# Pooling units side by side, and other places for the gate units' loads, one S4 product and the pooling weights

## The chip, the core and the metric

The kernel runs on one NeuronCore of one Trainium2 chip. The metric is the device time of one execution in microseconds; lower is better. TensorE (PE) multiplies matrices into PSUM, VectorE (DVE) and ScalarE (ACT) do the elementwise work, GpSimd (POOL) and SyncE (SP) mostly issue transfers (DMAs). Each engine has a queue of its own and works it off in the order in which it was written when the program was built; engines wait for each other, and for transfers, on semaphores.

## The reference

One layer of a sequence model: 512 positions, 1024 channels, float32.

```python
h = rms_norm(x, norm_mix)
u_pool, u_lru, q, k, v, g_logits = split(h @ w_in)        # 1024 columns each, g_logits 3 x 1024
gates  = sigmoid(g_logits + b_gate)                       # three branches
y_pool = per group g (windows 2, 4, 8, 16):  (mean over window - u) @ w_pool[g], times pool_scale
y_lru  = width-4 conv, two block-diagonal gates, a scan over positions
y_sb   = stick-breaking attention, 8 heads of 128, strictly causal
merged = gates0 * (y_pool @ w_branch0) + gates1 * (y_lru @ w_branch1) + gates2 * (y_sb @ w_branch2)
x = x + merged @ w_out
x = x + (silu(h2 @ w_ffn_gate) * (h2 @ w_ffn_up)) @ w_ffn_down
```

## The kernel before, in words

**Precision.** Every float32 factor is split into a high part (ACT copies it to `float32r`) and a low part (DVE subtracts), and a product is three matmuls: high with high, high with low, low with high (`mm3`, `product`). The weight halves `whi`, `wlo` have three buffers each, filled by `split_w` (lines 142 and 143).

**Seven products for eight.** The columns of `w_in` for v, k, q, for the pooling input and for the third branch's gates are multiplied by a seven-product scheme (Strassen's, in Winograd's form). A *unit* is one such 2 x 2 block problem; its seven products are called 11, 12, 21/22 sums S1 to S4, and 22. The sums of activations (T1 to T4) are made once. The sums of weights are made partly by GpSimd transfers that add in flight (`accum_op=ALU.add`, lines 197, 212, 242, 249) and partly by DVE (lines 206 and 211). For a pooling unit (`add_pool7`) the buffer "21" first receives block 21 plus block 22 (S1); when S1 has been split, block 11 is added to it (S2); when S2 has been split, block 12 is added (S4). Buffer "11" receives block 21 after product 11 has been split, which gives S3. So S1, S2 and S4 of one unit are a chain: split, added transfer, split, added transfer, split.

**The stages, in time.** After the first gates and the LRU projections come v, k and q (three units of large products, line 858), then the two pooling units (`cc` 0 and 1, products `ps_uy`, `ps_ux`), then the two units of the third branch's gates (units 3 and 4, products `ps_gy`, `ps_gx`; all of these at line 342). In the stage before, unit 0 of the pooling runs all its seven products, then unit 1. Each pooling unit has two PSUM pairs, Y and X, of four pairs in all. A running mean of each pooling half (`pool_mean`, DVE, lines 933 to 941) is queued in a background list `bg`, of which `tick` issues a piece after each product.

Then follow the branches: `branch(1, c)` (LRU output `yHH`, `yHL`, loaded by GpSimd at line 1250 into the buffers that held the activations) and `branch(0, c)` (pooling output), four chunks `c` each, two weight halves per chunk. The pooling's own small products (`pool_back`, `pps`) stand ahead of them in the program. Attention's 52 steps (`abg`, from `queue_attention`: per head a load, transposes, scores, weights' transposes, output) are spread between: each `tick` issues the next step. In the kernel before, `pool_back` ticks eight times, a chunk half of either branch ticks 1 + 2 times (`TICKS`), and `branch(0, c)` once more ahead of each chunk. After the branches comes the third branch's seven-product part (`b7`), the output projection and the FFN.

**What sets the order.** The text of the program gives each instruction a priority; `tc.high_priority(n)` moves a piece ahead by n instructions. When the program is built, a planner with its own cost estimates writes each engine's queue from these priorities, and it also chooses which freed buffer a new tile takes. `weights(key)` makes the splits of up to two products beyond the one in use. A transfer whose buffer is not yet free, or whose source is not yet written, holds up everything behind it in the queue of the engine that issues it.

**Buffers.** The pooling and gate blocks lie in eight buffers of tag "w" (`NAW`); unit 1's gate temporaries `gx1`, `gy1` take two of the same. Branch weights come in through three buffers of tag "raw" in the pool `wp`, and in the kernel before the pooling group weights `rawp` (line 1045) go through the same three, two groups at a time. The later stages have twelve load slots (`slot_ld`, tag "l") on the memory that the "w" buffers held before.

## Time and profile before

| | us |
|---|---|
| median of the runs | 901.07 (900.61 to 902.67, 3 runs) |
| profiled execution | 898.37 |
| its span, first to last instruction | 896.6 |
| PE busy | 867.5 (97%) |
| DVE busy | 745.3 (83%) |
| ACT busy | 528.5 (59%) |
| POOL busy | 96.6 (11%) |

The span is what the trace covers; the execution's own time is 1.8 us longer. Busy time of PE is counted over pipelined matmuls, so 97% doesn't mean that the array worked at its full rate: the granted clock (PEclk) has to be read beside it. The profile names instructions by their line and by out<-in of tile names without numbers, so `pw<-in_w_pool_dram` is a load or an added transfer of pooling blocks, and `qw<-in_w_gate_dram` one of a gate unit. `DVE pw` at lines 933 to 941 is a running mean, which happens to have the same name.

### The profile page before, as it was taken

What the parts mean: (1) busy time and instruction counts of PE and PEld (TensorE: products, weight loads), DVE (VectorE), ACT (ScalarE), POOL (GpSimd) and SP (SyncE); (2) the same over time, 40 slices, a digit from 0 to 9 for tenths busy, and PEclk for the clock granted to TensorE, in tenths of its full rate; (3) what the DMA queues carried; (4) which work ended last, traced back from release to release, by engine and by line L of the source; (5) the groups of instructions that cost most, each with busy time, mean ns of one, the idle gap of its engine ahead of it and who ended that gap; (6) DMA issues with size and microseconds to landing.
All of it is one profiled execution on the core that took longest, in us unless ns stands there. A gap on an engine that the chain in (4) does not pass through costs nothing.

```text
span 896.6 us, 14576 instructions
## 1 busy us (share of the span) xinstructions
PE 867.5 (97%) x5707; PEld 796.3 (89%) x5707; DVE 745.3 (83%) x947; ACT 528.5 (59%) x733; POOL 96.6 (11%) x139
## 2 busy tenths in 40 slices
PE   9999999999968988999999999999999999999998
PEld 6888878888858987879888998889999999999998
DVE  6799898989746874897998597689988889899974
ACT  6554998667834464776765454446555555755642
POOL 1110002232351012000000110000000000021300
PEclk9999999999979999999999999999999999999999
DMA  9586255998787638844564685427444333698923
GB/s 339 144 293 189 95 187 165 280 264 231 237 239 186 161 104 283 258 138 145 161 180 144 130 197 189 130 82 212 119 108 139 108 94 119 184 255 205 198 54 118
DMA packets 114725, 158.31 MB, mean 177 GB/s; under 512 B 8288, under 2 KB 86112, under 8 KB 114656
## 3 DMA queue, kind: packets, MB, share of 16 engines
q1 hardware_dynamic: 100832, 107.30, 37.4%
q0 software_dynamic: 13680, 49.81, 24.4%
q8 instruction: 45, 0.74, 0.3%
q10 hardware_dynamic: 144, 0.26, 0.1%
q14 instruction: 24, 0.20, 0.1%
HBM read 136.90 MB, written 18.87 MB: 174 GB/s over the span
## 4 chain that ended last, share of the span: by engine, by line
PE 79%; DVE 8%; ACT 5%; DMA 5%; issue 2%; POOL 0%; SPq 0%; DVEq 0%; ACTq 0%; POOLq 0%
PE ps_y L342 11%; PE ps_x L342 8%; PE ps_q L858 7%; PE ps_dy L1710 6%; PE ps_dx L1710 5%; DMA pw<-in_w_pool_dram 3%; PE ps_gate L761 3%; PE ps_bY L1334 2%; DVE wlo L143 2%; PE ps_br L334 2%; PE ps_br L335 2%; PE ps_br L333 2%; PE ps_gy L342 2%; PE ps_bX L1334 2%; PE ps_uy L342 2%
## 5 line engine op out<-in xcount | busy, mean ns | idle before, releaser
L142 ACT ACTIVATE whi<-raw 128x1024 fp32r<-128x1024 f32 x61 | 64.4, 1056 | 73.4 <-PE ps_out L334 15.5
L143 DVE TENSOR_TENSOR wlo<-raw,whi 128x1024 fp32r<-128x1024 f32 x61 | 74.3, 1219 | 25.7 <-ACT whi L142 25.4
L143 DVE TENSOR_TENSOR wlo<-qw,whi 128x1024 fp32r<-128x1024 f32 x48 | 58.2, 1217 | 17.5 <-ACT whi L142 17.5
L142 ACT ACTIVATE whi<-qw 128x1024 fp32r<-128x1024 f32 x48 | 50.4, 1053 | 32.9 <-PE ps_q L858 11.8
L1495 ACT ACTIVATE wh_S<-w_S 128x1024 fp32r<-128x1024 f32 x36 | 38.2, 1062 | 29.0 <-PE ps_y L342 20.4
L1616 POOL DMA_DIRECT2D dw<-in_w_down_dram x20 | 17.3, 883 | 304.4 <-DMA dw<-in_w_down_dram 253.3
L1496 DVE TENSOR_TENSOR wl_S<-w_S,wh_S 128x1024 fp32r<-128x1024 f32 x36 | 43.8, 1219 | 3.3 <-ACT wh_S L1495 3.3
L1495 ACT ACTIVATE wh<-w 128x1024 fp32r<-128x1024 f32 x27 | 28.7, 1062 | 27.7 <-PE ps_x L342 9.4
L1496 DVE TENSOR_TENSOR wl<-w,wh 128x1024 fp32r<-128x1024 f32 x27 | 32.9, 1220 | 7.9 <-ACT wh L1495 7.9
L1495 ACT ACTIVATE whdS<-dw 128x1024 fp32r<-128x1024 f32 x20 | 21.2, 1058 | 20.4 <-PE ps_dy L1710 10.6
L143 DVE TENSOR_TENSOR wlo<-pw,whi 128x1024 fp32r<-128x1024 f32 x14 | 16.6, 1221 | 18.5 <-ACT whi L142 18.5
L1496 DVE TENSOR_TENSOR wldS<-dw,whdS 128x1024 fp32r<-128x1024 f32 x20 | 24.1, 1219 | 4.9 <-ACT whdS L1495 4.9
L333 PE MATMUL ps_br<-yHH,whi 128*128 128x512 f32 x64 | 24.4, 384 | 2.6 <-DVE gy L921 1.3
L1141 DVE TENSOR_TENSOR_SCAN E<-K,ahead 128x512 f32<-128x512 f32 (+3 forms) x32 | 25.3, 812 | 1.4 <-ACT K L1137 1.4
L334 PE MATMUL ps_br<-yHL,whi 128*128 128x512 f32 x64 | 24.7, 386 | 1.8 <-DMA yHL<-ydl 1.8
L333 PE MATMUL ps_lru<-HH,whi 128*128 128x512 f32 x64 | 24.6, 384 | 0.0
L333 PE MATMUL ps_br<-yph,whi 128*128 128x512 f32 x64 | 24.5, 383 | 0.0
L335 PE MATMUL ps_br<-yHH,wlo 128*128 128x512 f32 x64 | 24.5, 383 | 0.0
L333 PE MATMUL ps_gate<-HH,whi 128*128 128x512 f32 x64 | 24.4, 381 | 0.0
L334 PE MATMUL ps_lru<-HL,whi 128*128 128x512 f32 x64 | 24.3, 379 | 0.0
L335 PE MATMUL ps_lru<-HH,wlo 128*128 128x512 f32 x64 | 24.3, 379 | 0.0
L334 PE MATMUL ps_gate<-HL,whi 128*128 128x512 f32 x64 | 24.3, 379 | 0.0
(778 smaller groups left out, 3551.6 us busy)
## 6 DMA issues: line engine op xcount, KB each, us to landing
qw<-in_w_qkv_dram SPq DMA_DIRECT2D x24, 512.0 KB, 7.5
raw<-in_w_in_dram SPq DMA_DIRECT2D x23, 512.0 KB, 5.2
dw<-in_w_down_dram POOLq DMA_DIRECT2D x20, 512.0 KB, 8.1
w<-in_w_ffn_gate_dram SPq DMA_DIRECT2D x36, 256.0 KB, 4.2
w<-in_w_ffn_up_dram SPq DMA_DIRECT2D x36, 256.0 KB, 4.7
raw<-in_w_branch_dram SPq DMA_DIRECT2D x16, 512.0 KB, 4.1
qw<-in_w_qkv_dram POOLq DMA_DIRECT2D x12, 512.0 KB, 8.3
qd<-r POOLq DMA_DIRECT2D x12, 512.0 KB, 7.4
```

Source lines behind the costliest of these rows:

```text
L142: act(hi, raw, AF.Copy)
L143: los.append(dve.tensor_tensor(lo, raw, hi.bitcast(F32), ALU.subtract).ins)
L333: nc.tensor.matmul(ps, lh, rh, start=start, stop=False, skip_group_check=skip)
L334: nc.tensor.matmul(ps, lh, rl, start=False, stop=False, skip_group_check=skip)
L335: nc.tensor.matmul(ps, ll, rh, start=False, stop=stop, skip_group_check=skip)
L342: nc.tensor.matmul(o, a_[a][:, w, k, :], il2(b_[b][:, k, :]), start=first and n == k == 0, stop=last and n == 2 and k == 3, skip_group_che ...
L761: nc.tensor.matmul(pss[n // 2][n % 2], w[:, k % 2, n * P:(n + 1) * P], il(hu[k][x_]), start=k == 0 and w is wh and x_ == 0, stop=k == KT - ...
L858: nc.tensor.matmul(ps[:, a, :], b_[:, k, ts_], il(a_[:, kk, :]), start=first and n == k == 0, stop=n == 2 and k == 3, skip_group_check=True)
L1334: nc.tensor.matmul(o, ah[x_][:, w, k, :], il2(b[k][y_]), start=first_ and n == k == 0, stop=n == 2 and k == 3, skip_group_check=True)
L1495: act(h, src, AF.Copy)
L1496: dve.tensor_tensor(l, src, h.bitcast(F32), ALU.subtract)
L1710: nc.tensor.matmul(o, a_[a][:, w, k0 + k, :], il2(b_[b][:, k, :]), start=first and i == k == 0, stop=last and i == 2 and k == nk - 1, skip ...
```

## The change

The pooling units' fourteen products are put in one order in which the two units alternate (`PORDER` now lists pairs of unit and product), with all four PSUM pairs in use at once. Gate unit 3's blocks are loaded at other products of the pooling stage, one buffer each. Gate unit 4 runs S4 before S3 (`UORDER`). The pooling group weights are loaded one group at a time into load slots, in place of two loads of two groups into the "raw" buffers. Attention's first four steps are issued ahead of the pooling's group products, these then tick once per group and not once per half; `branch(0, c)` ticks once and not 1 or 2 times after each half of the columns, so a chunk half of branch 1 issues three steps and one of branch 0 two.

```diff
--- before.py
+++ after.py
@@ -171,6 +171,7 @@
 
     ORDER = ("11", "12", "S2", "S1", "S3", "S4", "22")
     WITH = {"11": "11", "12": "21", "S2": "T2", "S1": "T1", "S3": "T3", "S4": "22", "22": "T4"}
+    UORDER = {4: ("11", "12", "S2", "S1", "S4", "S3", "22")}
     CH = {"11": 0, "12": 0, "21": 1, "22": 1}
     KH = {"11": 0, "12": 1, "21": 0, "22": 1}
     VKQ = (2, 1, 0)
@@ -227,7 +228,8 @@
     def add_then(f):
         specs[-1] = (specs[-1][0], lambda n, make=specs[-1][1]: (make(n), f())[0])
 
-    PORDER = ("11", "S1", "S2", "12", "S3", "S4", "22")
+    PORDER = ((0, "11"), (0, "S1"), (1, "11"), (1, "S1"), (0, "S2"), (0, "12"), (0, "S3"), (1, "S2"),
+              (0, "S4"), (0, "22"), (1, "12"), (1, "S3"), (1, "S4"), (1, "22"))
     PNEXT = {"11": ("11", "21"), "S1": ("21", "11"), "S2": ("21", "12")}
     praw = {}
 
@@ -247,8 +249,7 @@
             if nm in PNEXT:
                 buf, m = PNEXT[nm]
                 nc.gpsimd.dma_start(praw[u, buf], pool_src(u, m), accum_op=ALU.add)
-            if u:
-                seven_load(3, {"11": ("21", "11"), "S2": ("12",), "S3": ("22",)}.get(nm, ()))
+            seven_load(3, {(1, "S2"): ("11",), (0, "S4"): ("21",), (0, "22"): ("12", "22")}.get((u, nm), ()))
             return parts
         specs.append((("p7", u, nm), make))
 
@@ -264,10 +265,9 @@
     add_then(lambda: seven_load(0, ("21", "11", "12", "22")))
     for n, (u, pieces, _) in enumerate(UNITS):
         if n == 3:
-            for cc in range(2):
-                for nm in PORDER:
-                    add_pool7(cc, nm)
-        for nm in ORDER:
+            for cc, nm in PORDER:
+                add_pool7(cc, nm)
+        for nm in UORDER.get(n, ORDER):
             for i in range(pieces):
                 add_seven(n, nm, i)
     for br in BRANCHES[:2]:
@@ -940,28 +940,28 @@
                                          invpos[:, 0:w - 1], ALU.mult, ALU.mult)
                 dve.scalar_tensor_tensor(u, prev, 1.0 / w, u, ALU.mult, ALU.subtract)
 
-        for cc in range(2):
-            lo, hi = slice(0, H), slice(H, S)
-            Y = pb.tile([P, 2, S], F32, tag="mm", name=f"ps_uy{cc}")
-            X = pb.tile([P, 2, S], F32, tag="mm", name=f"ps_ux{cc}")
-            for j in range(2):
+        lo, hi = slice(0, H), slice(H, S)
+        plan = {"11": ("y", 1, True, 0, lo), "S1": ("x", 1, True, 1, hi), "S2": ("y", 1, False, 0, hi),
+                "12": ("x", 0, False, None, None), "S3": ("y", 1, False, 1, lo),
+                "S4": ("x", 1, False, None, None), "22": ("y", 0, False, None, None)}
+        banks = {}
+        for cc, nm in PORDER:
+            z, half, first_, j, ts_ = plan[nm]
+            if first_:
+                banks[cc, z] = pb.tile([P, 2, S], F32, tag="mm", name=f"ps_u{z}{cc}")
                 upool[cc, j] = mp.tile([P, 2, S], F32, tag="m", name=f"u{cc}{j}")
-            plan = {"11": (Y, 1, True, 0, lo), "S1": (X, 1, True, 1, hi), "S2": (Y, 1, False, 0, hi),
-                    "12": (X, 0, False, None, None), "S3": (Y, 1, False, 1, lo),
-                    "S4": (X, 1, False, None, None), "22": (Y, 0, False, None, None)}
-            for nm in PORDER:
-                ps, half, first_, j, ts_ = plan[nm]
-                product(weights("p7", cc, nm), BQ[WITH[nm]], ps, half, first_, True)
-                if j is not None:
-                    with tc.high_priority(EARLY):
-                        act(two2(upool[cc, j][:, :, ts_]), in_order2(ps[:, :, hi]), AF.Copy,
-                            scale=-1.0 if j else 1.0)
-                elif nm != "12":
-                    j = int(nm == "22")
-                    v = two2(upool[cc, j])
-                    dve.tensor_tensor(v, v, in_order2(ps), ALU.subtract if j else ALU.add)
-                    bg.append(lambda cc=cc, j=j: pool_mean(cc, j))
-                tick(1)
+            ps = banks[cc, z]
+            product(weights("p7", cc, nm), BQ[WITH[nm]], ps, half, first_, True)
+            if j is not None:
+                with tc.high_priority(EARLY):
+                    act(two2(upool[cc, j][:, :, ts_]), in_order2(ps[:, :, hi]), AF.Copy,
+                        scale=-1.0 if j else 1.0)
+            elif nm != "12":
+                j = int(nm == "22")
+                v = two2(upool[cc, j])
+                dve.tensor_tensor(v, v, in_order2(ps), ALU.subtract if j else ALU.add)
+                bg.append(lambda cc=cc, j=j: pool_mean(cc, j))
+            tick(1)
 
         for cc in range(2):
             tx, ty = (b4([2, S], f"g{n}{cc}", "bw"[cc]) for n in "xy")
@@ -978,7 +978,7 @@
                     "S3": (Y, 1, False, ty, lo, Y, hi),
                     "S4": (X, 1, False, None, None, None, None),
                     "22": (Y, 0, False, None, None, None, None)}
-            for nm in ORDER:
+            for nm in UORDER.get(3 + cc, ORDER):
                 ps, half, first_, t, ts_, src, ss = plan[nm]
                 product(weights("seven", 3 + cc, nm, 0), BQ[WITH[nm]], ps, half, first_, True)
                 if t is not None:
@@ -1040,15 +1040,13 @@
         pool_p = {}
         pool_w = {}
 
-        def load_pool_weights(h):
-            raw = wp.tile([P, 4, 256], F32, tag="raw", name=f"rawp{h}")
-            nc.sync.dma_start(raw, w_pool[2 * h:2 * h + 2].rearrange("g (k p) c -> p (g k) c", p=P))
-            for g in range(2):
-                hi, lo = slot_r(f"wph{h}{g}", (2, 256)), slot_r(f"wpl{h}{g}", (2, 256))
-                r = raw[:, 2 * g:2 * g + 2, :]
-                act(hi, r, AF.Copy)
-                dve.tensor_tensor(lo, r, hi.bitcast(F32), ALU.subtract)
-                pool_w[2 * h + g] = (hi, lo)
+        def load_pool_weights(g):
+            raw = slot_ld(f"rawp{g}", (2, 256))
+            nc.sync.dma_start(raw, w_pool[g].rearrange("(k p) c -> p k c", p=P))
+            hi, lo = slot_r(f"wph{g}", (2, 256)), slot_r(f"wpl{g}", (2, 256))
+            act(hi, raw, AF.Copy)
+            dve.tensor_tensor(lo, raw, hi.bitcast(F32), ALU.subtract)
+            pool_w[g] = hi, lo
 
         def pool_split(g, j):
             u = upool[g // 2, j][:, g % 2, :]
@@ -1079,7 +1077,7 @@
                 gts = gate_load(br, c)
             if br == 0:
                 tick()
-            merge(br, c, chan_chunk(("br", br, c), rhs, TICKS), gts)
+            merge(br, c, chan_chunk(("br", br, c), rhs, TICKS if br else 1), gts)
 
 
         ysb = {}
@@ -1232,15 +1230,17 @@
         queue_attention()
         abg[0]()
         abg[0] = nothing
+        tick(4)
         for h in range(2):
-            load_pool_weights(h)
+            for g in (2 * h, 2 * h + 1):
+                load_pool_weights(g)
             for g in (2 * h, 2 * h + 1):
                 for j in range(2):
                     pool_split(g, j)
         for g in range(4):
             for j in range(2):
                 pool_back(g, j)
-                tick()
+            tick()
 
         ylru = []
         for i in range(2):
```

## The prediction

> **What bounds the kernel now.** I read the page first, then the waits of PE, then busy time by stretch, then the chain and the queues inside the stretches that stand out.
>
> ```profile
> span 896.6 us, 14576 instructions
> PEclk9999999999979999999999999999999999999999
> PE 79%; DVE 8%; ACT 5%; DMA 5%; issue 2%; POOL 0%; SPq 0%; DVEq 0%; ACTq 0%; POOLq 0%
> ```
>
> PE carries the chain that ends last; DMA has 5% of it, which for a PE-bound kernel is time at which the array stood still. So a gain can only come from waits of PE and from lost clock. The waits of PE (who, for whom, us in total, times, longest):
>
> ```profile
> PE ps_uy L342 <- ACT whi L142: 9.3, 2, 7.8
> PE ps_gx L342 <- DVE wlo L143: 2.9, 2, 2.2
> PE pw L1154 <- DVE A L1143: 2.6, 3, 1.4
> PE ps_br L334 <- DMA yHL<-ydl: 1.8, 1, 1.8
> PE ps_br L333 <- DVE gy L921: 1.3, 1, 1.3
> PE ps_br L333 <- DMA yHH<-ydh: 1.3, 1, 1.3
> PE ps_uy L342 <- DVE wlo L143: 1.2, 2, 0.8
> PE pq L1104 <- DVE wtl L1157: 1.2, 2, 0.7
> ```
>
> These are 21.6 us, all in the stages that the change touches: pooling (`ps_uy`), gate units (`ps_gx`), the step to the branches (`ps_br`), attention (`pw`, `pq`). The stretches (busy us of PE, PEld, DVE, ACT, POOL; then clock, DMA share, GB/s):
>
> ```profile
> 251.16:253.84 2.68, 2.68 (x26) 2.68 (x25) 1.55 (x3) 1.06 (x1) 2.68 (x5) 1.00 0.63 142
> 251.20:303.80 52.60, 42.11 (x337) 41.24 (x336) 30.77 (x40) 19.54 (x23) 16.71 (x18) 0.87 0.78 196
> 303.80:326.40 22.60, 19.62 (x171) 19.05 (x171) 20.00 (x27) 10.16 (x12) 0.86 (x1) 1.00 0.26 45
> 326.40:345.50 19.10, 19.07 (x170) 18.77 (x168) 12.23 (x11) 13.43 (x18) 4.30 (x8) 1.00 0.72 219
> 345.50:358.00 12.50, 8.12 (x35) 6.51 (x36) 4.25 (x5) 3.95 (x6) 4.18 (x10) 1.00 1.05 340
> 436.70:482.90 46.20, 43.40 (x244) 37.88 (x243) 44.45 (x85) 30.83 (x68) 1.78 (x2) 1.00 0.48 140
> 482.90:498.50 15.60, 15.60 (x75) 13.67 (x74) 10.55 (x20) 5.57 (x12) 1.72 (x2) 1.00 0.79 210
> ```
>
> The first row is one unstalled product: 2.68 us. Fourteen pooling products would take 37.5; they take 52.6, so 15.1 are lost. The gate units take 41.7 for the same 37.5, 4.2 lost, nearly all in unit 3, where DVE is busy 20.0 of 22.6. At the start of the branches 12.50 - 8.12 = 4.4 are lost. In branch 0 DVE is busy 96%, PE 2.8 short; the last 15.6 us of it have no attention left.
>
> Part of the loss is clock:
>
> ```profile
> 259.00:262.40 3.40, 0.00 (x0) 0.00 (x0) 0.00 (x0) 0.00 (x0) 2.98 (x6) 0.50 1.05 217
> 286.30:289.70 3.40, 1.26 (x9) 1.07 (x9) 2.06 (x2) 3.15 (x4) 0.54 (x1) 1.00 0.00 0
> 289.70:293.10 3.40, 3.40 (x19) 3.40 (x18) 3.40 (x7) 0.29 (x1) 0.33 (x1) 0.50 0.75 108
> 358.00:361.40 3.40, 3.37 (x9) 2.19 (x8) 1.41 (x2) 2.50 (x4) 0.00 (x0) 0.50 1.10 308
> ```
>
> After 3.4 us in which PE was busy only 1.26, the clock stood at 0.50 for the next 3.4 us: 1.7 us of work lost. The same follows the branch stall (358.0 to 361.4), so that step costs 4.4 + 1.7 = 6.1.
>
> Why pooling waits is in the chain (start, us, what), and in POOL's queue (start, us; in brackets the idle time before and what ended it; the last row but one is PE's, the last the landing times of all these transfers):
>
> ```profile
> 241.47 8.83 DMA pw<-in_w_pool_dram
> 252.79 10.46 DMA pw<-in_w_pool_dram
> 263.34 1.06 ACT whi L142
> 348.98 8.30 DMA yHL<-ydl
> ```
>
> ```profile
> 250.90 0.88 POOL L242 DMA_DIRECT2D pw<-in_w_pool_dram  x1 [7.30 <-DMA pw<-in_w_pool_dram]
> 252.21 2.12 POOL L249 DMA_DIRECT2D pw<-in_w_pool_dram  x2
> 255.36 5.45 POOL L369 TENSOR_TENSOR qrs<-qss,mhalf 128x32 f32<-128x32 f32 x1 [0.29 <-DVE qss L844]
> 265.95 0.92 POOL L249 DMA_DIRECT2D pw<-in_w_pool_dram  x1 [3.46 <-DVE wlo L143]
> 273.28 0.87 POOL L197 DMA_DIRECT2D qw<-in_w_gate_dram  x1 [6.41 <-DMA qw<-in_w_gate_dram]
> 264.45 0.58 PE L342 MATMUL ps_uy<-hT2h,whi 128*128 128x256 f32 x1 [7.77 <-ACT whi L142]
> DMA to landing us min/median/max: 4.9/6.0/10.5
> ```
>
> Unit 0's S2 needs the transfer issued at 252.79, which takes 10.46 us, then a split. Products 11 and S1 have ended at 251.16 + 2 x 2.68 = 256.5, and S2 starts at 264.45: 7.8 us idle, then half clock.
>
> **The change part by part.** *The pooling order.* No matmul, split or transfer is added or removed. Ahead of (0, S2) now stand (1, 11) and (1, S1), 5.36 us of work. (1, S1)'s added transfer is the one issued at 250.90, before the critical one; at the median of 6.0 it lands at 256.9, and (1, S1) starts at 259.2. PE then ends (1, S1) at 261.9. The critical transfer is issued at 252.79 as before, since what precedes it on POOL is the same, so S2 starts at 264.45: 2.6 us idle instead of 7.8. Whether clock goes with it is uncertain: 2.6 idle can leave 0.8 busy in a 3.4 us stretch (then it does, 1.7) or be divided between two; I take half, 0.9. After that each chain link of a unit has three to four products, 8 to 11 us, in place of one to three: S4's transfer is issued at 265.95 as now, and S4's product stands at 264.45 + 4 x 2.68 = 275.2, 9.2 us later. For unit 1 the transfer for S2 waits for POOL's power instruction (5.45 us from 255.36; the 3.46 of idle time before 265.95 puts the end of it and the small ones behind at 262.5); nothing shows its new landing. At the 10.46 seen, it lands at 273, 0.5 after (1, S2) wants to start with a split still to come, so up to 2; at the median of 6.0 it lands at 268.5 and is hidden. Two units' transfers share the stretch, but unit 0's are through by then, so I take the median. Pooling loses 2.6 + 0.9 = 3.5 instead of 15.1: **11.6 gained**; bounds 8.4 (full clock drop, and one more transfer of 512 KB ahead of the critical one, 2.4 us at the 217 GB/s of 259.0 to 262.4) and 12.5 (no clock drop).
>
> *A rule on the clock.* The profile's row shows half clock after a stretch with 1.26 us of work in it. The Trainium skill (TensorE: Matmul & The Clock Gate, Part 1: The HAM clock gate) says that the array falls to half rate after at least one idle window of about 3.4 us and recovers after one busy window. By it the 2.6 us wait would cost no clock and the forecast would be 0.9 us faster; the row disagrees, since PE was at work for a third of that stretch, so I keep the 0.9.
>
> *Gate unit 3's loads* (SP, and the adding transfer on POOL that now waits at 273.28 for its load for 6.41 us, holding POOL's queue). They are four loads and one adding transfer before and after; each now goes into a buffer freed just before it, and the add stands behind (0, S4) instead of (1, 11). Cost nothing: the products that need them begin at about 292, and the latest is issued after (0, 22), about 15 us earlier. If the cover went, its price would be one landing, the 8.83 above.
>
> *DVE.* The same running means now come in a shorter time:
>
> ```profile
> L937 DVE TENSOR_TENSOR_SCAN pw<-u,pw 128x508 f32<-128x508 f32 (+2 forms) x6 | 7.5, 1257 | 0.0
> L941 DVE SCALAR_TENSOR_TENSOR u<-pw,u 128x512 f32<-128x512 f32 x8 | 5.4, 681 | 0.0
> 277.90:346.80 68.90, 62.35 (x532) 61.09 (x530) 54.23 (x67) 33.89 (x41) 10.54 (x16) 0.98 0.58 153
> ```
>
> From the end of (0, S4) to the first instruction of the branches DVE has 54.2 us of work, and 68.9 us for it now; afterwards, without stalls, it is 277.9 to 292.2 + 37.5 + 1.3 = 331, 53 us. Of the work 12.9 us (7.5 + 5.4) and some small ones are running means, which PE doesn't need there, and DVE is idle 8.2 us right behind (12.50 - 4.25), so the stretch isn't bound by DVE, but its queue is fixed and a split will stand behind a scan more often than now. I take 1.5 more than today's 4.2 **(-1.5)**; bounds +2 and -5 (the 2.9 of waits for `wlo` disappear, or come twice more).
>
> *S4 before S3 in unit 4.* S4 is the last reader of the second half of the activations, whose buffers take `yHH` and `yHL`. It ends 2.68 us earlier against the end of the gates, and so do its DVE and ACT steps and its store. The last of four loads stands behind a gate store that waits for the last product (issue 348.98, 8.30 us, PE waits 1.8 for it); if the planner writes all four ahead of that store, it goes out some 5 us earlier and both waits and the half clock go. The 1.3 for the PSUM pair of `gy` stays, unless the head's transposes, now ahead in the program, fill it. I take 1.5 left of 6.1: **4.6 gained**; bounds 0 and 6.
>
> *Pooling weights.* Two loads of two groups (128 x 1024 f32, 512 KB) become four of one: two more issues on SP.
>
> ```profile
> 342.38 0.38 SPq L1045 DMA_DIRECT2D rawp<-in_w_pool_dram  x1
> ```
>
> That is 0.8 us of SP, hidden. They no longer hold "raw" buffers back from the branch weights, but wait for "w" buffers to be left. No wait of PE above is for branch weights, so nothing is gained; taken as 0, and the bound on the other side is the slower rival below.
>
> *Attention steps.* 8 + 24 + 28 ticks for 52 steps become 8 + 24 + 20: the same work, in 62 us of branch 0 instead of 46. DVE's 44.45 + 10.55 us then fill 89%. PE's waits for `A` and `wtl` (2.6 + 1.2) and the 2.8 that PE is short shrink; the tail now ends with branch 0, but its first taker, the third product of `b7` or later, comes some 8 us after. **2 gained**, bounds 0 and 4.
>
> Sum: 11.6 - 1.5 + 4.6 + 2 = 16.7. The profiled execution took 898.37, 2.7 below the median of 901.07; that gives 881.7 for such an execution and 884.4 for the median.
>
> **The rivals.** *All hidden:* no clock drop, no DVE stall, the branch step and attention at their bounds: 12.5 + 2 + 6 + 4 = 24.5, 876.6. For it: every wait has a named cause that is moved. Against: DVE's 96%.
>
> *The adds collide.* Unit 1's two adds enter POOL's transfer queue behind unit 0's, and each link then takes the 10.46 seen rather than the median of 6.0; (0, S2) and (1, S2) both wait. Pooling gains 5 to 8 less: 891. For it: DMA share 1.05 and nothing on PE in 259.0 to 262.4. The Trainium skill (DMA: Bandwidth & Descriptors, Issuing engines are not separate DMA queues) says that transfers of all engines share the same DMA engines; the trace agrees with that 1.05, and 10.46 us for one transfer.
>
> *DVE becomes the bound* between the pooling and the branches: 54.2 us of work in 53, splits late throughout, 5 us and a half clock: 16.7 - 6 = 10.7, 890.
>
> *Slower.* The pooling weights sit behind buffers of the gates' temporaries, whose last store goes out here:
>
> ```profile
> 348.45 0.54 POOL L925 DMA_DIRECT2D gd<-gy  x1 [1.61 <-ACT gy L923]
> ```
>
> With the 8.30 of its neighbour it lands about 357, 11 us after the gates. If the planner writes the pooling products first on PE, PE waits for that, and for a load, 8 more; its products then overlap with the splits of the groups. 19 us idle and two half-clock stretches at 1.7 are 22 instead of 6. The rest gives 12.1, so 901.07 + 16 - 12.1 = 905. It decides when this stall passes 18 us. Against it: now PE's queue has branch products first, and the planner can take buffers of weights split earlier.
>
> *No effect:* the planner already writes, or undoes, the order; 901.
>
> **How the numbers follow.** The forecast 0.50, own range 879 to 889; all hidden 0.13; adds collide 0.15; DVE 0.13; slower 0.06; none 0.03. The range goes from 876.6 to 895, which takes in the collided case at its worst and leaves out under 2 in 10. Faster by over 0.2% (about what this measurement can tell) is 0.91, within 0.03, slower 0.06.
>
> **What would show it.** Right: (0, S2) starts within 3 us of the end of (1, S1), pooling lasts 39 to 42 us, waits of `ps_br` for `yHH` and `yHL` gone, attention reaching to the end of branch 0. Wrong: `ps_uy` still waiting over 5 us, more `wlo` waits in the gates than 6 us, PE waiting for `wph` or `p00h`, or SP standing still ahead of the branch weights.

## The result, and the profile after

The changed kernel takes 889.88 us (median of 4 runs, 889.18 to 891.19); the kernel before took 900.84 beside it. The ratio is 0.988, with a 95% interval of 0.986 to 0.990: 11 us faster, where 16.7 were forecast, and 5.5 us above the predicted 884.4. The profiled execution of the changed kernel took 890.54, that of the kernel before 898.37; the two differ by 7.8 us, since the one lies a little above its median and the other below. Two lines of the page first: the span, and the chain's shares.

```profile
span 888.8 us, 14571 instructions
...
PE 80%; ACT 6%; DVE 6%; DMA 4%; issue 2%; POOL 1%; SPq 0%; DVEq 0%; ACTq 0%; POOLq 0%
```

PE still carries the chain, and DMA still has 4% of it. The waits of PE in the changed kernel (who, for whom, us in total, times, longest):

```profile
PE z L333 <- ACT A L1136: 4.4, 1, 4.4
PE ps_gy L342 <- ACT gy L985: 2.7, 1, 2.7
PE ps_uy L342 <- ACT whi L142: 2.7, 1, 2.7
PE ps_gy L342 <- ACT gx L985: 2.2, 2, 1.5
PE ps_gx L342 <- DVE wlo L143: 1.5, 1, 1.5
...
PE ps_uy L342 <- ACT u L957: 0.8, 1, 0.8
...
PE ps_uy L342 <- DVE wlo L143: 0.8, 1, 0.8
```

The 9.3 us that `ps_uy` waited for `whi` have become 2.7. PE no longer waits for `yHH` and `yHL`, nor in `pw`, and `pq` waits 0.2 us for `wtl`. Three waits are new: `z`, the attention scores of head 0, waits 4.4 us for ACT, and `ps_gy` waits for ACT's copies, 2.7 us for that into `gy` in unit 4 and 2.2 for two into `gx`. The stretches of pooling and gate units, and three single ones of 3.41 us (busy us of PE, PEld, DVE, ACT, POOL; then clock, DMA share, GB/s):

```profile
248.82:293.01 44.19, 39.88 (x337) 39.19 (x336) 27.19 (x34) 19.57 (x23) 16.94 (x18) 0.96 0.88 228
293.01:338.98 45.97, 39.45 (x338) 38.12 (x337) 35.75 (x44) 23.35 (x29) 6.96 (x13) 1.00 0.52 130
...
263.39:266.80 3.41, 2.92 (x13) 2.92 (x14) 2.89 (x3) 2.53 (x4) 0.90 (x1) 0.50 1.09 256
348.73:352.14 3.41, 0.23 (x2) 0.00 (x0) 0.55 (x1) 0.03 (x1) 0.00 (x0) 1.00 0.70 184
352.14:355.55 3.41, 2.18 (x7) 1.91 (x8) 1.71 (x3) 2.25 (x6) 0.00 (x0) 0.50 0.88 275
```

Cut in the same way in both traces (from the first product of each stage to the first of the next), the time went like this:

| stage, us | before | after |
|---|---|---|
| start to the first pooling product | 251.16 | 248.82 |
| pooling | 52.67 | 44.19 |
| gate units | 41.48 | 45.97 |
| step to the branches | 1.48 | 1.55 |
| branch 1 and the pooling weights | 89.94 | 88.74 |
| branch 0 | 61.61 | 58.80 |
| `b7`, output | 79.29 | 79.29 |
| the rest | 318.98 | 321.41 |

Pooling gave 8.5 us and branch 0 2.8. The gate units cost 4.5. The 1.2 of the branch-1 row is what is left of a larger gain, since the branch stall went and another one, at `z`, came. The first and the last row lie outside the change: in the kernel before, the clock reached full speed at 9.8 us of the span, in the changed kernel at 4.0; and of the 2.4 us at the end, 1.5 are two waits of `ps_dx` at 811 us that only some profiles have (see the end).

The new stall can be followed in the chain of work (start, us, what). Time runs downwards; each row is what released the next:

```profile
333.39 1.06 ACT whi L142
334.44 1.23 ACT gx L923 x2
335.67 0.49 ACT gy L985
...
336.20 2.96 PE ps_gy L342 x24
...
342.14 6.30 DMA gd<-gy
...
348.57 0.37 SPq L1095
...
348.99 3.10 DMA rawp<-in_w_pool_dram
...
352.11 0.63 ACT wph L1047
352.74 0.59 ACT A L1136
...
353.37 0.58 PE z L333
```

The load of head 0's V (`at`, L1095) got the buffer that the second gate temporary of unit 4 (`gy`) had, so SP held it back until `gy` was stored, at 348.44. Behind it on SP stood the four `rawp` loads, whose own buffers were free by then: with V on another queue (below) they go out some 6 us earlier. The first landed at 352.09; on ACT the split of that weight (`wph`) stands ahead of `A`, and `A` has to leave the PSUM bank that `z` wants. So a buffer's last store reached PE by way of SP's order and ACT's order: 4.4 us idle and then two stretches at half clock (2.18 and 3.42 us of work, 2.8 lost). The first four rows are the other new wait, read below.

### The profile page after: what moved, and what is told of

Same layout as the page of the kernel before. It is cut to its first block, busy times and chain, and to the rows that moved or that the text cites. A ratio compares the mean times of both kernels' runs of the same rounds, so it can differ in the third digit from the quotient of the medians.

```text
span 888.8 us, 14571 instructions
## 1 busy us (share of the span) xinstructions
PE 863.5 (97%) x5707; PEld 794.9 (89%) x5707; DVE 744.7 (84%) x947; ACT 528.2 (59%) x733; POOL 96.7 (11%) x139
## 4 chain that ended last, share of the span: by engine, by line
PE 80%; ACT 6%; DVE 6%; DMA 4%; issue 2%; POOL 1%; SPq 0%; DVEq 0%; ACTq 0%; POOLq 0%
PE ps_y L342 11%; PE ps_x L342 8%; PE ps_q L858 7%; PE ps_dy L1710 5%; PE ps_dx L1710 4%; PE ps_br L334 3%; PE ps_br L335 3%; PE ps_br L333 3%; PE ps_bY L1334 2%; PE ps_gate L761 2%; PE ps_gy L342 2%; DMA pw<-in_w_pool_dram 2%; PE ps_bX L1334 2%; DVE wlo L143 2%; ACT whi L142 1%
## 5 line engine op out<-in xcount | busy, mean ns | idle before, releaser
L142 ACT ACTIVATE whi<-pw 128x1024 fp32r<-128x1024 f32 x14 | 14.8, 1059 | 21.9 <-DMA pw<-in_w_pool_dram 14.1
```

Of the source, the lines that this page charges most:

```text
L142: act(hi, raw, AF.Copy)
```

## The experiments

The intervals below are plus or minus 0.2 to 0.35%, so a difference between two variants of under some 3.5 us is not settled by their times (an estimate from two such intervals). There the text goes by the traces, of which each variant has one.

**The pooling order alone.** The kernel before, with the pooling loop, its PSUM pairs and the four loads of gate unit 3 as in the change, and everything else as it was. The start of the edit against the kernel before:

```diff
-            for cc in range(2):
-                for nm in PORDER:
-                    add_pool7(cc, nm)
+            for cc, nm in PORDER:
+                add_pool7(cc, nm)
...
```

> The kernel before with the new order of the pooling products alone: the PSUM pairs for two units at once and the four loads of gate unit 3 in their new places; unit 4, the pooling weights and the attention steps as before. The theory: in the two traces pooling went from 52.67 to 44.19 us, 8.5 shorter, and the gate units from 41.5 to 45.97, of which the 2.74 us wait of unit 4's 22 for ACT's snapshot belongs to S4 before S3, which isn't here. So this kernel gains 8.5 less some 1.5 to 2 in the gates, and the waits of ps_br for yHL and yHH (1.8 and 1.3 in the profile before) are back: 893 to 895 on the scale of 900.8 for the kernel before. The rival, that the order of the pooling products carries the whole measured gain of 11 and the other parts cancel: 890. If the other parts carry most of it, 897 or more.

Measured: 893.38 against 900.69, ratio 0.992 (0.990 to 0.995), 7.3 us of the 11. The pooling stage took 45.24, the gate units 42.63. The branch stall is back, and now the pooling's small products (`pps`) wait there too (waits of PE; then a row of ACT with the idle time before it in brackets):

```profile
PE pps L332 <- DVE ypl L1067: 2.0, 1, 2.0
PE ps_br L333 <- DMA yHL<-ydl: 1.8, 1, 1.8
...
PE ps_br L332 <- DMA yHH<-ydh: 1.4, 1, 1.4
```

```profile
347.75 1.06 ACT L142 ACTIVATE whi<-raw 128x1024 fp32r<-128x1024 f32 x1 [8.10 <-DMA raw<-in_w_branch_dram]
```

The last of the pooling weights had landed at 337.58; their splits stand on ACT behind that of a branch weight, which came late. In this profile, the slowest of the eight executions (896.72), the stage of branch 1 took 96.63, 6.7 more than before, and most of the 7.4 of the pooling stage was lost again there. By the medians the interleaved order is still the largest part of the gain; the gate units lose little by it (41.48 before).

**S3 before S4 again.** The changed kernel with `UORDER = {}`.

```diff
-    UORDER = {4: ("11", "12", "S2", "S1", "S4", "S3", "22")}
+    UORDER = {}
```

> The changed kernel with unit 4's products in the old order, S3 before S4. The theory: the 2.74 us in which 22 of unit 4 waits for ACT's snapshot behind S3 (one PSUM pair's half is copied between the two products) goes, since S4 stands between them again, and the waits of ps_br for yHH and yHL, up to 1.3 and 1.8 us in the profile before, come back at the step to the branches, where the PE wait of the changed kernel is 1.55: between 1.5 us faster and 1.5 us slower than the changed kernel, 888.4 to 891.4. The prediction's step (4.6 us gained by S4 before S3) says 4 us slower or more: 893 to 895. A wait for the pooling weights (4.4 us for z) that is as long as before here would say that it does not hang on this order.

Measured: 888.11, ratio 0.987 (0.983 to 0.990); against the changed kernel's 0.988 this is no difference. The gate units fall from 45.97 to 42.62, and what S4 first had removed is back (waits of PE):

```profile
PE ps_br L334 <- DMA yHL<-ydl: 2.8, 1, 2.8
...
PE z L333 <- ACT A L1136: 2.0, 1, 2.0
```

The edit trades one wait for another: with S4 first, the end of S3 and the start of 22 stand back to back on the same PSUM pair, and 22 must wait until ACT has copied S3's half. (PE's queue in the changed kernel has 13 of S3's 24 matmuls ahead of S4 and 11 behind it.)

**Two loads exchanged.** Nothing but which of 21 and 11 of gate unit 3 is loaded first; the compiler then gives `gx` the buffer that V takes later, and the store of `gx` lands some 5 us before that of `gy` (343.6 and 348.4 in the changed kernel).

```diff
-            seven_load(3, {(1, "S2"): ("11",), (0, "S4"): ("21",), (0, "22"): ("12", "22")}.get((u, nm), ()))
+            seven_load(3, {(1, "S2"): ("21",), (0, "S4"): ("11",), (0, "22"): ("12", "22")}.get((u, nm), ()))
```

> The changed kernel with two of gate unit 3's loads exchanged: 21 behind (1, S2) and 11 behind (0, S4). Nothing else differs in the program, but by the compiler's placement the first gate temporary of unit 4 (gx) and the second (gy) exchange their buffers, and the load of head 0's V (at) then takes the buffer of gx, as in the kernel before. The theory that SP stands still ahead of the pooling weights because that load waits for gy's store (it landed at 348.44 in the changed kernel, at 343.6 the store of gx): at is issued some 4.9 us earlier, rawp0 lands at about 347, and the 4.41 us wait of z and most of the 3.4 us of half clock behind it go: 883 to 886. The rival, that rawp comes late since the transfers of this stretch fill the DMA engines, or that ACT reaches the split late anyway: no change, 889 to 891.

Measured: 886.52, ratio 0.985 (0.981 to 0.988). The same rows of its chain:

```profile
344.31 0.55 SPq L1095
344.90 6.29 DMA rawp<-in_w_pool_dram
351.22 0.63 ACT wph L1047
```

V goes out 3.2 us after the last gate product instead of 9.6, `z` waits 1.3 us, no half clock follows, and the branch-1 stage falls from 88.74 to 83.94. On ACT the split still stands ahead of `A`, as in the changed kernel, so this is the clean test of the stall: counted from the end of the gates, `rawp` lands 3.0 us earlier (10.1 instead of 13.1), and the wait is 3.1 shorter. The cause holds. The amount was smaller than expected, because `rawp` now takes 6.29 us to land where it took 3.10: it left earlier, into a stretch in which the store of `gy`, a load of branch weights and V itself were in flight. The gate units took 48.46, 2.5 more than in the changed kernel: a wait for `wlo` is 0.9 longer, and the rest is half clock behind a wait that both have; the last section says why.

**The pooling weights loaded as before,** two loads through the "raw" buffers, ahead of V on SP.

```diff
-            raw = slot_ld(f"rawp{g}", (2, 256))
-            nc.sync.dma_start(raw, w_pool[g].rearrange("(k p) c -> p k c", p=P))
+            raw = wp.tile([P, 4, 256], F32, tag="raw", name=f"rawp{h}")
+            nc.sync.dma_start(raw, w_pool[2 * h:2 * h + 2].rearrange("g (k p) c -> p (g k) c", p=P))
...
```

> The changed kernel with the pooling weights loaded as before, two loads of two groups through the raw buffers, which stand ahead of at on SP. The theory (rawp late because its issue stands behind at on SP): the 4.4 us wait of z at 353.4 and half clock behind it go, 883 to 887, unless the branch weights, whose raw buffers these loads now hold, are late in turn (this would show as waits of ps_br for their splits, 1 to 3 us). The prediction's step, that this part of the change is worth 0: 890.

Measured: 892.51, ratio 0.991 (0.988 to 0.994). A miss, and not on the branch weights' products but ahead of them: the "raw" buffers held the branch weights back on SP, and ACT, in its fixed order, waited for one of those with the activation of `gy` and both `qkh` behind it. One row of SP and one of ACT (start, us; in brackets the idle time before):

```profile
336.19 13.40 SPq L149 DMA_DIRECT2D raw<-in_w_branch_dram  x2
```

```profile
346.88 1.06 ACT L142 ACTIVATE whi<-raw 128x1024 fp32r<-128x1024 f32 x1 [10.40 <-DMA raw<-in_w_branch_dram]
```

`z` waits 2.7 us for `qkh` and 3.0 for `A`. So the old place costs a stall as well as the new one, and the two nearly cancel: the stage of branch 1 takes 89.25 here and 88.74 in the changed kernel. The 2.6 us between the medians are not settled.

**Early snapshots.** ACT's copies of the gate units get the priority that the pooling's have.

```diff
                 if t is not None:
-                    act(two2(t[:, :, ts_]), in_order2(src[:, :, ss]), AF.Copy)
+                    with tc.high_priority(EARLY):
+                        act(two2(t[:, :, ts_]), in_order2(src[:, :, ss]), AF.Copy)
```

> The changed kernel with ACT's snapshots of the gate units at the priority that the pooling's snapshots have, so that ACT takes S3's snapshot of unit 4 before the two activations of gx (1.32 us, 334.35 to 335.67 in the changed kernel). The theory: 22 of unit 4 waits for ACT's queue, not only for the snapshot itself: S3's snapshot starts at about 334.2 in place of 335.57, the 2.74 us wait shrinks to about 1.4, the same as for gx in the units (1.5). The wait of z for the pooling weights stays (SP is still held by gy's store, which goes out some 1.3 us earlier too): 888 to 889.5. The rival, that the snapshot's own way from PE to ACT and back is the 2.7: no change.

Measured: 888.62, ratio 0.986 (0.983 to 0.989). The wait is as expected:

```profile
PE ps_gy L342 <- ACT gy L986: 1.5, 1, 1.5
```

In the changed kernel S3 ends at 333.46. ACT has then just begun the split of a later weight (`whi`, 333.39 in the chain above), does the two activations of `gx` (334.44, 1.23 us) and then the copy (335.67). With early snapshots the activations come behind the copy, but the split still stands ahead of it (rows of ACT; S3 ends at 331.87 here, and 22 starts at 333.39):

```profile
331.79 1.06 ACT L142 ACTIVATE whi<-raw 128x1024 fp32r<-128x1024 f32 x1 [0.16 <-PE ps_gy L342]
332.76 0.58 ACT L986 ACTIVATE gy<-ps_gy 128x512 f32<-128x512 f32 x1
```

So the activations cost 1.2 of the 2.7, and the other 1.5 are 0.9 of the split and 0.6 for the copy.

**Exchanged loads and early snapshots together.**

> Both edits together: the two loads of gate unit 3 exchanged and the early snapshots. The theory takes the two waits as independent: with the exchanged loads 886.5 was measured, its profile has the 2.74 us wait of ps_gy and 3.4 us of half clock right behind it (337.4 to 341). With the wait cut to 1.4 the half clock can go as well: 1.4 to 3 less, 883.5 to 885. If the rival of the early snapshots holds: 886.5.

Measured: 888.74, ratio 0.986 (0.983 to 0.989): no gain on either edit alone. The wait for `gy`'s copy is 1.5, and no half clock follows it. Its chain shows where the shorter gates went:

```profile
345.16 0.37 SPq L1096
345.58 6.67 DMA rawp<-in_w_pool_dram
352.27 0.63 ACT wph L1048
```

The whole of this trace lies 1.3 us later when S3 ends (335.32 against 334.03 with exchanged loads alone), so times are counted from there. The gates ended after 4.3 us instead of 7.1. `rawp` landed after 16.9 instead of 17.2, hardly sooner, since `gx`'s activations now stand behind the copy and its store, for which V waits, went out 0.5 later. So PE stood 3.9 us at `z` instead of 1.3, and half clock followed: a shorter gate stage only reached the same wait sooner.

**Exchanged loads, S3 before S4.**

> The exchanged loads with unit 4's old order, S3 before S4: with the run of the exchanged loads alone it measures S4 before S3 where SP isn't held. The theory: the order costs the 2.7 us wait for the snapshot and gains the waits for yHH and yHL and the half clock behind them (0.3 + 2.8 us and two stretches of half clock in the run of the old order on the changed kernel, the second of which belongs to the wait for the pooling weights): 886 to 889, that is 0.5 faster to 2.5 slower than the 886.5 of the exchanged loads. The prediction's step says 4.6 slower: 891.

Measured: 888.70, ratio 0.987 (0.984 to 0.990). PE waits 2.9 us for `yHL` and 1.9 for `A`; the gate units take 42.63. With SP held for less time, S4 first is worth 2.2 by the medians; it was worth -1.8 with SP held. Both are inside what the times can tell. Over the gates and branch 1 together the traces give 0.0 here and -1.2 there: the edit is worth about 0.

**The attention steps of before.** Both edits to the steps undone.

```diff
-            merge(br, c, chan_chunk(("br", br, c), rhs, TICKS if br else 1), gts)
+            merge(br, c, chan_chunk(("br", br, c), rhs, TICKS), gts)
...
-        tick(4)
...
                 pool_back(g, j)
-            tick()
+                tick()
```

> The changed kernel with the attention steps of before: no four at the start, one behind each of the eight half groups, three a chunk half in both branches. The theory: branch 0 goes from 58.80 back to the 61.61 that it took in the kernel before and with the new pooling order alone, and the stage with branch 1 and the pooling weights gets at most 1 us shorter or longer, its waits being for the pooling weights: 2 to 3.5 slower, 892 to 893.5. The prediction's step says 2 (0 to 4). The rival, that the gain in branch 0 is only moved out of branch 1, where four steps were added: 890.

Measured: 896.15, ratio 0.995 (0.993 to 0.997), 6 us slower than the changed kernel, about twice what was expected. Its waits of PE:

```profile
PE pps L333 <- ACT p00h L1013: 4.8, 1, 4.8
...
PE pw L1152 <- DVE A L1141: 2.6, 3, 1.4
PE pq L1102 <- DVE wtl L1155: 1.6, 3, 0.7
```

Branch 0 is back at 61.61, and branch 1 takes 91.65 instead of 88.74. The pooling weights are as late as in the changed kernel; PE meets that wait at `pps` (4.8 us) where the changed kernel meets it at `z` (4.4). Most of the 2.9 are the waits for DVE in the attention steps, which are back here as in branch 0: 1.8 us more in branch 1 (379 to 400 us) than in the changed kernel.

**V on POOL's queue.** The same wait for the same store, with nothing of SP behind it.

```diff
-                        nc.sync.dma_start(r, qd[t, g][:, hd].rearrange("(b p) c -> p b c", p=P))
+                        q = nc.gpsimd if h == 0 and t == 2 else nc.sync
+                        q.dma_start(r, qd[t, g][:, hd].rearrange("(b p) c -> p b c", p=P))
```

> The changed kernel with one load on another queue: head 0's V (at) is issued by POOL in place of SP, behind POOL's small fills, so that it still waits for gy's store but no longer with the four rawp loads behind it. The theory (one queue in order: in the changed kernel the load of V was issued 0.1 us after gy's store had landed, and rawp0 0.4 us behind it): the rawp loads go out right behind the three loads of branch weights, about 2 us before the end of the gates in place of 10 behind it, and even at the 6.7 us that rawp0 took to land with the exchanged loads they are there some 8 us ahead of the split; the 4.41 us wait of z goes, and so do the two stretches of half clock behind it (3.4 us lost): 881 to 884.5. The rival, that these loads only trade places with those of the branch weights and of yHH and yHL on the DMA engines: waits of 2 to 4 us for those in place of that for z, 888 to 891.

Measured: 888.29, ratio 0.986 (0.984 to 0.988). The 4.4 us at `z` are gone, as expected; the time is that of the rival (888 to 891), but without the waits that it named. Two things of the expectation were wrong. The `rawp` loads went out 3.1 us after the gates, not 2 before them, since the third load of branch weights, which waits for a buffer of its own, stands ahead of them on SP and went out at 2.7. And the wait came back at the next taker. POOL's rows, DVE's, and PE's wait:

```profile
349.37 0.78 POOL L1096 DMA_DIRECT2D at<-qd  x1 [4.52 <-DMA gd<-gy]
350.16 0.31 POOL L1035 TENSOR_SCALAR_AFFINE_SELECT ahead<-ahead 128x128 bf16<-128x128 bf16 x1
```

```profile
350.50 1.23 DVE L1140 TENSOR_TENSOR_SCAN E<-K,ahead 128x512 f32<-128x512 f32 x1 [1.97 <-ACT wph L1047]
...
354.82 0.67 DVE L1014 TENSOR_TENSOR p00l<-u,p00h 128x512 fp32r<-128x512 f32 x1
```

```profile
PE pps L334 <- DVE p00l L1014: 2.9, 1, 2.9
```

The load moved its wait with it: a fill of 0.31 us (`ahead`) now stood behind it on POOL, the scan that reads it began 0.03 us after that fill had ended (the bracket names another releaser, which had been done for a while), and the splits for `pps` stood behind the scan on DVE.

One thing more differs from the changed kernel: the planner wrote `A` ahead of the first split of the pooling weights on ACT, not behind it.

```profile
348.27 0.68 ACT L1137 ACTIVATE A<-z,qrs 128x512 f32<-128x512 f32 x1
348.84 0.63 ACT L1047 ACTIVATE wph<-rawp 128x512 fp32r<-128x512 f32 x1
```

Here this matters little, as the weight had landed at 348.50. But it means that this variant and the three below don't test SP's order alone: the wait at `z` can go by ACT's order as well.

**The same with early snapshots.**

> The same with the early snapshots of the gate units. The theory: the 2.74 us wait of unit 4's 22 falls to 1.5 as in the run of the early snapshots alone (there 1.5 was measured), and nothing else waits for it: 1.2 to 3 less than the load of V on POOL alone (the upper end where the half clock that can follow the wait goes too), 879.5 to 883. The rival, from the run with exchanged loads and early snapshots (888.7, no gain over the exchanged loads alone): no change against the load of V on POOL alone.

Measured: 886.52, ratio 0.983 (0.981 to 0.986). The gates' wait is 1.5 and their stage 44.74 instead of 47.59; PE waits 2.5 us for `p00h` in place of 2.9 for `p00l`. The size expected for the whole was missed for the reason just given; the 1.8 us against V on POOL alone are inside the 1.2 to 3 expected, and not settled by the times.

**V on POOL behind the fills.** V's load stays on POOL, and POOL's two fills of `ahead` are moved ahead of it.

```diff
-        nc.gpsimd.memset(ahead, 0.0)
+        with tc.high_priority(400):
+            nc.gpsimd.memset(ahead, 0.0)
...
-        nc.gpsimd.affine_select(out=d, in_=d, compare_op=ALU.not_equal, fill=1.0, base=0,
-                                pattern=[[-1, P]], channel_multiplier=1)
+        with tc.high_priority(400):
+            nc.gpsimd.affine_select(out=d, in_=d, compare_op=ALU.not_equal, fill=1.0, base=0,
+                                    pattern=[[-1, P]], channel_multiplier=1)
```

> The load of V on POOL, with POOL's two fills of ahead (a memset and an affine_select) put in front of it. In the run without this the affine_select stood behind V's load, which waited until gy's store had landed (issued at 349.37, 4.52 us of POOL standing still, the affine_select at 350.16), so that DVE's scan E, whose input K was there at 348.96, began at 350.50, the splits wpl and p00l behind it on DVE came at 352.44 and 354.82, and PE waited 2.86 us for p00l, with a stretch of half clock behind it. The theory: all of this follows from the one row on POOL; with the fills in front E starts at about 349.0, p00l 1.5 us earlier or more, and PE's wait for pps falls to 0 to 1.4 us and mostly takes the half clock (1.7) with it: 1.5 to 4.5 less than that run, 883.8 to 886.8. The rival, that p00l is late because DVE has too much work there: 888.

Measured: 883.55 (881.73 to 884.93), ratio 0.981 (0.979 to 0.983): the fastest of all and just faster than expected, 16.8 us below the kernel before (900.31 beside it). Its interval lies below that of the changed kernel; that of the next variant touches it. Two POOL rows, the waits of `pps`, and the stretch from the last gate product to branch 0:

```profile
341.63 0.31 POOL L1037 TENSOR_SCALAR_AFFINE_SELECT ahead<-ahead 128x128 bf16<-128x128 bf16 x1
...
347.81 0.80 POOL L1098 DMA_DIRECT2D at<-qd  x1 [4.78 <-DMA gd<-gy]
```

```profile
PE pps L333 <- ACT p00h L1013: 1.2, 1, 1.2
...
PE pps L334 <- DVE p00l L1014: 0.4, 1, 0.4
```

```profile
337.32:423.14 85.82, 83.18 (x457) 71.59 (x456) 71.22 (x104) 58.44 (x108) 3.35 (x8) 1.00 0.67 204
```

POOL still stands still for 4.78 us, and now nobody is behind it. The stage of branch 1 and the pooling weights (84.27 us, from the first branch product at 338.87) has no half clock left. It is no shorter than with the two loads exchanged (83.94); that variant lost its time in the gates (48.46 against 45.98). Of the 8.8 us between the profiled executions of the changed kernel and of this one, 4.5 stand in this stage; 1.9 stand in pooling, which had no half clock this time, and 2.7 behind the branches, and nothing was edited in those two. ACT's order counts here: `A` ran at 346.19, and the first `rawp` landed at 348.44, so behind the split `A` would have come some 2.8 us later (an estimate from these rows).

**And with early snapshots.**

> The same with the early snapshots of the gate units. The theory: rawp0 landed 3 us later in the run with both (12.1 us behind the end of the gates against 9.1), so the splits of the pooling weights still stand behind it on ACT and PE may wait 1 to 2.5 us for p00h; the gates are 1.2 to 2.8 us shorter: 882.5 to 886, and no slower than without the early snapshots. The rival: what the gates gain is lost again at the pooling weights, which then are as late as before in time: the same as without the early snapshots within 1 us.

Measured: 884.28, ratio 0.984 (0.981 to 0.986). The rival holds here: gates 1.2 us shorter, 1.9 us of wait for `p00h` instead of 1.2, and a stretch of half clock behind it. With nothing waiting behind V on SP or POOL, the landing of the pooling weights sets that place, and a shorter gate stage only reaches it sooner.

## Why the prediction was right, and where it was not

The direction and the whole range held; the sum was 5.7 too large, and the time missed the forecast's own range (879 to 889) by 0.9. It lies next to the 890 and 891 of two rivals, neither of which happened as told: PE waited neither for unit 1's adds nor longer for DVE's splits. That the total came this close is partly luck, since the terms were off in both directions. Of the signs named beforehand, (0, S2) and the waits for `yHH` and `yHL` came out; pooling took 44.19 where 39 to 42 were named, and SP did stand still, ahead of the pooling weights.

*The pooling order (11.6 gained).* The mechanism came out as worked out: (0, S2) waits 2.7 us instead of the 2.6 forecast, and no product of unit 1 waits for its adds. That was not because the transfers kept apart, as the forecast took it: in the pooling stage they landed after 8.5 us in the median and 13.9 at most, where 6.0 was taken. The products between the links of each chain covered that. The size was 8.5 in the trace, just above the lower bound of 8.4: the clock fell for a whole stretch (2.92 us of work, 1.5 lost, 0.9 taken), and two short waits of 0.8 each (`u`, `wlo`) were in no term. The pooling order alone gives 7.3 in the time of the whole.

*DVE in the gates (-1.5).* The gates did lose more, 4.5 where 1.5 was taken, but not to DVE: its `wlo` waits fell from 2.9 to 1.5. The pooling order alone costs the gates 1.2, close to the term, but by ACT: 2.2 of waits for its copies into `gx` are new. The larger part belongs to the step that failed, *S4 before S3 in unit 4*, which was costed only at the branch end. It was said what S4 sooner frees, and not what then stands next to what: S3 and 22 share a PSUM pair, and S4 had been the work between them that hid ACT's copy. In its place 22 waits 2.7. Its branch side was right in every point: `yHH` and `yHL` wait no more, no half clock follows there, the step takes 1.55. Counted with the 2.7 at the gates and the 2.8 and 2.0 that return without it, the 4.6 were about 0.

*Pooling weights (0).* This failed, and the "slower" rival had named how: SP behind the last store of the gates' temporaries. That store landed 9.5 us after the gates (11 forecast). The stall was 4.4 us with 2.8 of half clock, not 19 and 3.4, because PE had branch products ahead, as the argument against that rival said. What the rival left out is the other side: in the "raw" buffers the old loads hold up the branch weights, which costs nearly the same. The forecast also took the exchange of two loads of gate unit 3 for nothing; PE never waited for them as loads, but their order decides which temporary lies in the buffer that V needs.

*Attention steps (2, bounds 0 to 4).* In branch 0 it came out as told, with 2.8 gained. But undoing both edits costs 6 by the medians and 5.7 in the two branch stages, above the bounds, since PE's waits for DVE (`A`, `wtl`) come back in branch 1 as well, where the sum had nothing. Which of the two edits frees those isn't shown.

The 16.8 us of the last variant are close to the 16.7 of the sum. That is chance: it doesn't confirm the terms, which were off in both directions. What the held-up load of V cost is 4.5 us by the stage of branch 1 and 6.3 by the medians, with ACT's order changed as well.

## What to carry to other kernels

When a load gets another buffer, look up who had that buffer last, when its store lands, and which loads stand behind on the same queue: the exchanged loads, and V on POOL without and with the fills in front, are 3.4, 1.6 and 6.3 us faster here than the changed kernel by their medians, of which only the last is settled by the times. Moving the waiting load to another queue moves its wait too, so look behind it there as well. When a product is moved up, look at the two that then become neighbours: if they share a PSUM pair, nothing hides the copy between them any more, nor what stands ahead of the copy on its engine.

## What was not expected of the hardware

The clock. In the 14 profiles, half clock between 200 and 510 us came in pieces of 3.41, 6.83 or 10.24 us. All clock changes of a trace lie on one grid of 3.413 us. On these grids, 29 of the 31 stretches at full clock in which PE was busy for less than 48% were followed by half clock, and none of the 103 in which it was busy for 48 to 85%. The same wait of 2.74 us of unit 4's 22 falls on both sides. In the changed kernel the grid cuts it in two:

```profile
331.66:335.07 3.41, 1.80 (x17) 1.61 (x15) 2.73 (x3) 2.74 (x4) 1.60 (x3) 1.00 0.38 101
335.07:338.49 3.42, 2.29 (x20) 2.29 (x21) 0.76 (x1) 1.08 (x2) 1.06 (x2) 1.00 0.88 208
```

and with the two loads exchanged it lies in one piece:

```profile
334.29:337.70 3.41, 0.93 (x8) 0.93 (x9) 2.11 (x2) 2.43 (x4) 1.36 (x3) 1.00 0.95 245
337.70:341.11 3.41, 3.41 (x19) 3.41 (x18) 0.00 (x0) 0.00 (x0) 0.00 (x0) 0.50 1.03 315
```

So waits that add up to some 1.8 to 3.4 us cost nothing more or 1.7 and more, by where the grid happens to lie. How much of the spread between executions comes from this is open: with the lost clock (one minus the granted clock, times the time) taken off each execution, the spread of the kernel before halves (13 runs, standard deviation 2.6 to 1.3 us), and that of the pooling order alone doesn't shrink (8 runs, 2.0 to 2.2). The Trainium skill (TensorE: Matmul & The Clock Gate, Part 1: The HAM clock gate) says that the window is about 3.4 us long and free-running, which these rows bear out; it says that half rate comes after at least one idle window, and here a window that was nearly half busy was enough. The prediction took half a loss for a wait of 2.6 us; of the 13 profiles with the new pooling order 8 had a loss there, 3 one behind the wait for `u` that follows, and 2 none.

How long a load takes depends on when it leaves: the same 256 KB of `rawp` landed after 3.1 us behind the store of `gy`, after 6.3 us when they left just behind it with the store still in flight, and after 6.7 and 8.0 us in two other variants, the store in flight as well. The Trainium skill (DMA: Bandwidth & Descriptors, Issuing engines are not separate DMA queues) says that queues of different engines share the DMA engines; these landings agree, without showing which of the transfers in flight cost how much.

Left open: the two waits of `ps_dx` at 811 us, 1.5 us together, one or both of which stand in 4 of the 14 profiles, in a stage that no variant changed; and what else the variants with two edits lose beyond their waits, where the difference is within the runs' spread.
